# The prologue of a DiT block: modulation by channel pairs, with four projections beside it

## The chip, the core and the metric

The kernel runs on one core of one Trainium2 chip. The metric is the device time of one execution in microseconds; the median of three runs of the kernel before is 1344.03 us (1343.78 to 1344.9). Its engines: PE (TensorE, matmuls into the accumulators in PSUM), ACT (ScalarE), DVE (VectorE), POOL (GpSimd) and SP (SyncE, which here only issues transfers). Each engine works through its own queue in order.

## The reference, cut to what matters

One layer over 1024 latent tokens and 256 context tokens, width 1024, all in float32:

```
m = silu(c) @ w_mod + b_mod          # six vectors of 1024 for the latents; the same with c_ctx for the context
h = rms_norm(x) * g0 * (1 + m[1]) + m[0]
p = h @ w_in                          # 3584 columns: q, two gates, v, g (512 each), and 2 x 512 for the recurrent group
# four HGRN2 heads of 128 columns, eight RG-LRU blocks, output projection, residual, SwiGLU, residual
```

Only m[0] (shift) and m[1] (scale) are needed before the first projection; they come from the first 2048 columns of w_mod. The other four vectors come later.

## The kernel before

Tokens are cut into three blocks: block 0 and 1 of 512 latent tokens, block 2 of the 256 context tokens. Channels are cut into eight k-tiles of 128. A float32 product at fp32r speed is done as three matmuls (`mm3`): both operands are split into a high and a low part (`split`: a cast on ACT, a subtraction on DVE), and hi x hi, hi x lo and lo x hi are added in PSUM. PSUM has eight accumulators: four of tag mm (`ps_mm`) and four of tag px (`ps_x`).

The prologue has these steps, with their lines:

- `load_wm` (L188 to L191) loads k-tile k of the 2048 columns of w_mod as two transfers of 512 KB, three tiles deep. The order on SP is written out by hand (L193 to L207): two k-tiles, block 0 of x, the other k-tiles with the nine small parameter vectors between them, then a tile of w_in, x of block 1, a second w_in tile, the context, the masks.
- L208 to L217: for each k-tile and each quarter of 512 columns, wm is split (L123, L124) and multiplied by `c4`, whose four columns are the high and low parts of the two silu'd vectors; four accumulators `pm` stay open over all k-tiles. The last k-tile is done by plain fp32 matmuls with `c2` (L211).
- `norm_x(b)` (L170 to L176): per 128 tokens a Square with sum on ACT, mean and root (DVE, POOL), a scaling on DVE. `turn(b, k)` (L178 to L183) transposes a k-tile of a block on PE, four transposes for a block of 512. Block 0 is evacuated into `xa` by ACT (L221).
- L225 to L259: the parameters of the recurrent group and of the gates (a chain of small operations on DVE, with three activations on ACT, called the lambda chain below).
- L261 to L275: `pm` is copied to `mrow`, 16 small transposes (L269) bring it into columns, and bias and gain are added: `mcol`.
- L276 to L287: for each block and k-tile, high part `hh` (ACT, L285), full value `hf` (DVE, L286), low part `hl` (DVE, L287).

`inproj(c0, blocks, evac)` (L151 to L160) then does 128 columns of w_in for some blocks: `prep_w` loads and splits the weights (`raw`, `whi`, `wlo`), 24 matmuls a block go into one accumulator, and `evac` takes it out. Head 0 asks for q (blocks 0 and 1), two gates and v (blocks 0, 1, 2). From there on the modulation rows of the later stages (`mod_rows`) are done in small steps on DVE with a sum over partitions by a matmul with ones (L304).

Apart from the order on SP, and one on DVE at the very end, the order on each engine comes from the planner of the tile framework: it takes instructions by program order as priority, places a later one earlier when by its own costs the earlier would have to wait, and puts tiles into free buffers of their tag. `manual_schedule(engines=...)` keeps the instructions traced inside it in the written order on the named engines.

Of the kernel before, what the change touches and what calls it, by code (L numbers as in the profile page):

```python
# [48 lines left out]
def block_kernel(ctx: ExitStack, tc: tile.TileContext, x, c, cx, c_ctx, w_mod, b_mod, norm_g, w_in, lb_logits, gnorm,  # L49
# [45 lines left out]
    # silu of the two conditioning vectors, as columns (k-tile, vector)  # L95
# [6 lines left out]
    c2 = const.tile([P, KD, 4], F32, name="c2")  # L102
    V.memset(c2[:, :, 2:4], 0.0)
    V.tensor_mul(c2[:, :, 0:2], cs.rearrange("p (v k) -> p k v", v=2), cc.rearrange("p (v k) -> p k v", v=2))
    c4 = const.tile([P, KD, 4], F32R, name="c4")
    S.activation(c4[:, :, 0:2], c2[:, :, 0:2], AF.Copy)
    V.tensor_sub(c4[:, :, 2:4], c2[:, :, 0:2], c4[:, :, 0:2].bitcast(F32))
# [26 lines left out]
    # ------------------------------------------------------------------ modulation, norm, input projection, mixers  # L134
# [7 lines left out]

    def prep_w(c0):
        raw = wpool.tile([P, KD, P], F32, tag="raw", name="raw", bufs=2)
        SP.dma_start(raw, w_in[:, c0:c0 + P].rearrange("(k p) f -> p k f", p=P))
        hi = wpool.tile([P, KD, P], F32R, tag="whi", name="whi", bufs=2)
        lo = wpool.tile([P, KD, P], F32R, tag="wlo", name="wlo", bufs=2)
        split(hi, lo, raw)
        prepped[c0] = hi, lo
# [12 lines left out]
    with pool("st") as st:  # L162
# [22 lines left out]
        pm = [ps_mm() for _ in range(4)]  # L185
        wms = []

        def load_wm(k):  # L188
            wms.append(st.tile([P, 2, D], F32, tag="wm", name="wm", bufs=3))
            for n in range(2):  # L190
                SP.dma_start(wms[k][:, n, :], w_mod[k * P:(k + 1) * P, n * D:(n + 1) * D])  # L191

        with tc.manual_schedule(engines={nc.sync.engine}):  # L193
            load_wm(0)
            load_wm(1)
            load_x(0)
            for k in range(2, KD):
                load_wm(k)
                for dst, src in small[2 * k - 4:2 * k - 2]:
                    SP.dma_start(dst, src)  # L200
            prep_w(0)
            load_x(1)
            prep_w(HW_)
            load_x(2)
            mk = st.tile([P, 7 * P], F32, name="mk")
            SP.dma_start(mk, masks)
        for k in range(KD):  # L207
            for n in range(4):  # L208
                wk = wms[k][:, n // 2, n % 2 * 512:(n % 2 + 1) * 512]
                if k == KD - 1:  # L210
                    PE.matmul(pm[n][:4, :], c2[:, k, :], wk, start=(k == 0), stop=(k == KD - 1))  # L211
                    continue
                wh = st.tile([P, 512], F32R, tag="wmh", name="wmh", bufs=3)
                wl = st.tile([P, 512], F32R, tag="wml", name="wml", bufs=3)
# [3 lines left out]
        norm_x(0)  # L218
        xa = st.tile([P, KD, 512], F32, name="xa")
        for k in range(KD):  # L220
            S.activation(xa[:, k, :], turn(0, k), AF.Copy)  # L221
        pt = ps_x()
        PE.transpose(pt[:, :NR], rows, ident[:NR, :NR])
        V.tensor_copy(cols, pt[:, :NR])

        # 8 * log_sigmoid(lambda)
        la = const.tile([P, 8], F32, name="la")
        lg = const.tile([P, 8], F32, name="lg")
        ls = const.tile([P, 8], F32, name="ls")
        ls2 = const.tile([P, 8], F32, name="ls2")  # L230
        lp = const.tile([P, 8], F32, name="lp")
        S.activation(la, col("lam", 0, 8), AF.Abs)
        S.activation(lg, la, AF.Sigmoid, scale=-1.0)
        V.tensor_scalar(ls, lg, -1.0, 2.0, op0=ALU.mult, op1=ALU.add)
        V.reciprocal(ls, ls)
        V.tensor_mul(ls, ls, lg)
        V.tensor_mul(ls2, ls, ls)
        V.tensor_scalar_mul(lp, ls2, 1.0 / 17.0)
        for n in (15, 13, 11, 9, 7, 5, 3):
            V.scalar_tensor_tensor(lp, lp, 1.0 / n, ls2, op0=ALU.add, op1=ALU.mult)  # L240
        V.scalar_tensor_tensor(lp, lp, 1.0, ls, op0=ALU.add, op1=ALU.mult)
        V.tensor_scalar_min(la, col("lam", 0, 8), 0.0)
        V.scalar_tensor_tensor(la, lp, -2.0, la, op0=ALU.mult, op1=ALU.add)
        loga = const.tile([P, 8], F32, name="loga")
        nloga = const.tile([P, 8], F32, name="nloga")
        V.tensor_scalar_mul(loga, la, 8.0)
        V.tensor_scalar_mul(nloga, la, -8.0)

        # lower bounds: softmax over the depth axis, cumulated, less its first layer
        lbe = const.tile([P, 8], F32, name="lbe")  # L250
        lbr = const.tile([P, 8], F32, name="lbr")
        lb = const.tile([P, 8], F32, name="lb")
        omlb = const.tile([P, 8], F32, name="omlb")
        V.tensor_sub(lbe, col("lb", 0, 8), col("lb", 0, 8))
        S.activation(lbe, lbe, AF.Exp)
        V.reciprocal(lbr, lbe)
        V.tensor_mul(lbe, lbe, lbr)
        V.tensor_sub(lb, lbe, lbe)
        V.tensor_scalar(omlb, lb, -1.0, 1.0, op0=ALU.mult, op1=ALU.add)  # L259

        mrow = st.tile([4, 2 * D], F32, name="mrow")  # L261
        for n in range(4):
            if n % 2:
                V.tensor_copy(mrow[:, n * 512:(n + 1) * 512], pm[n][:4, :])
            else:
                S.activation(mrow[:, n * 512:(n + 1) * 512], pm[n][:4, :], AF.Copy)
        pt = ps_x()
        for j in range(16):
            PE.transpose(pt[:, 4 * j:4 * j + 4], mrow[:, j * P:(j + 1) * P], ident[0:4, 0:4])  # L269
        mcol = st.tile([P, 16, 2], F32, name="mcol")  # L270
        ptv = pt[:, 0:64].rearrange("p (j h v) -> p j h v", h=2, v=2)
        V.tensor_copy(mcol, ptv[:, :, 1, :])
        V.tensor_add(mcol, mcol, ptv[:, :, 0, :])
        V.tensor_add(mcol, mcol, col("bm", 0, 16).unsqueeze(2).to_broadcast([P, 16, 2]))
        V.scalar_tensor_tensor(mcol[:, 8:16, :], mcol[:, 8:16, :], 1.0, col("g0", 0, 8).unsqueeze(2).to_broadcast([P, 8, 2]),  # L275
                               op0=ALU.add, op1=ALU.mult)  # L276
        for b in range(3):
            n = BL[b][1]
            v = b // 2
            if b:  # L280
                norm_x(b)
            for k in range(KD):
                src = turn(b, k) if b else xa[:, k, :]
                hf = st.tile([P, 512], F32, tag="hf", name="hf", bufs=3)
                S.activation(hh[b][:, k, :], src, AF.Identity, bias=mcol[:, k, v:v + 1], scale=mcol[:, 8 + k, v:v + 1])  # L285
                V.tensor_scalar(hf[:, :n], src, mcol[:, 8 + k, v:v + 1], mcol[:, k, v:v + 1], op0=ALU.mult, op1=ALU.add)  # L286
                V.tensor_sub(hl[b][:, k, :], hf[:, :n], hh[b][:, k, :].bitcast(F32))  # L287
# [66 lines left out]
    def rg_gates():  # L354
        # two diagonal blocks to a channel tile
# [94 lines left out]
    # ---------------- HGRN2 heads  # L450
    def hg_unit(h):
# [40 lines left out]
        # context state of both directions  # L492
# [24 lines left out]
        # intra-chunk scores by a binary tree over the chunk  # L517
# [41 lines left out]
        # chunk states  # L559
# [67 lines left out]
    with pool("rgp", "right") as cur[0]:  # L627
# [3 lines left out]
        for t in range(4):  # L631
            # gate; then the next tile's convolution goes before this one's scans
# [18 lines left out]
    for k in range(KD):  # L651
        # the mixers' rows, RG-LRU first
# [444 lines left out]
```

## Time and profile before

| | |
|---|---|
| median of three runs | 1344.03 us |
| profiled execution, span from first to last instruction | 1342.8 us |
| PE busy / DVE / ACT | 1294.6 / 978.2 / 655.3 us |
| SP's queue moved | 150.63 MB of 153.57 |

The profiled execution's own time is not listed beside its span; against the median there are 1.2 us around the span. PE's busy share is near full in all of the 40 slices but the first two and the last. In the views below, "busy" of a line is the time of its instructions on their engine, and "idle before, releaser" says what ended the engine's waiting. PEclk is the granted clock of TensorE, 1.00 at 2.4 GHz.

### The profile page before, as it was taken

The page shows a single profiled execution, that of the slowest core. Times are in us where ns is not written, and L with a number is a line of the kernel's source. Part 1 is how long each engine was busy: PE and PEld are TensorE (multiplying, and loading weights), DVE is VectorE, ACT ScalarE, POOL GpSimd, SP SyncE. Part 2 cuts the span into 40 slices and gives each one's busy share as a digit, 9 for nine tenths or more (in the row PEclk, how much of TensorE's full clock was granted, in tenths as well). Part 3 has the DMA queues.
Part 4 walks back from the last instruction along what each step waited for, and adds up shares of the span by engine and source line. Part 5 has one row for each costly group of instructions (what it writes and reads, how often), then busy time and mean ns, then how long its engine had stood idle before and what let it go on. Part 6 is the DMA issues. An engine that isn't in the chain of part 4 may idle for free.

```text
span 1342.8 us, 17344 instructions
## 1 busy us (share of the span) xinstructions
PE 1294.6 (96%) x6271; PEld 1050.8 (78%) x6271; DVE 978.2 (73%) x1609; ACT 655.3 (49%) x1168; POOL 37.7 (3%) x69
## 2 busy tenths in 40 slices
PE   6899999999999999999999999999999999999997
PEld 2587877888888877777887788888888888888886
DVE  5888769738467789874569867777666677896695
ACT  7762443534525777845767333333323334454552
POOL 0100000000000000000010000000000000000000
PEclk8899999999999999999999999999999999999999
DMA  8644042210101011166450532333233215953363
GB/s 301 217 155 160 26 149 64 80 33 17 32 17 32 17 48 47 55 209 206 132 166 25 172 96 88 100 118 110 86 112 104 91 71 188 384 158 95 101 212 102
DMA packets 112896, 153.57 MB, mean 114 GB/s; under 512 B 9469, under 2 KB 69218, under 8 KB 112810
## 3 DMA queue, kind: packets, MB, share of 16 engines
q1 hardware_dynamic: 112250, 150.63, 34.4%
q0 software_dynamic: 560, 1.84, 0.4%
q8 instruction: 49, 0.80, 0.3%
q14 instruction: 37, 0.30, 0.1%
HBM read 119.64 MB, written 32.80 MB: 114 GB/s over the span
## 4 chain that ended last, share of the span: by engine, by line
PE 77%; DVE 12%; ACT 6%; issue 2%; DMA 2%; POOL 1%; SPq 0%; POOLq 0%; DVEq 0%; ACTq 0%
PE mm L129 15%; PE mm L127 15%; PE mm L128 15%; PE px L127 7%; PE px L129 7%; PE px L128 7%; PE px L542 3%; DVE ii L443 1%; DMA raw<-in_w_out 1%; PE px L581 1%; DVE ii L435 1%; DVE a L430 1%; PE mm L217 1%; DVE th L431 1%; PE px L566 1%
## 5 line engine op out<-in xcount | busy, mean ns | idle before, releaser
L123 ACT ACTIVATE wh<-r 128x512 fp32r<-128x512 f32 x160 | 100.9, 633 | 250.8 <-PE mm L128 130.6
L127 PE MATMUL mm<-hh,whi 128*128 128x512 f32 (+1 forms) x576 | 216.1, 376 | 2.8 <-ACT hh L285 2.8
L128 PE MATMUL mm<-hl,whi 128*128 128x512 f32 (+1 forms) x576 | 214.8, 373 | 0.4 <-DVE hl L287 0.4
L129 PE MATMUL mm<-hh,wlo 128*128 128x512 f32 (+1 forms) x576 | 213.9, 374 | 1.0 <-DVE wlo L124 1.0
L127 PEld LDWEIGHTS mm<-hh,whi 128*128 128x128 f32 x576 | 109.2, 190 | 24.2 <-issue 4.3
L129 PEld LDWEIGHTS mm<-hh,wlo 128*128 128x128 f32 x576 | 109.2, 190 | 18.9 <-issue 1.7
L128 PEld LDWEIGHTS mm<-hl,whi 128*128 128x128 f32 x576 | 109.3, 190 | 17.3 <-DVE hl L287 1.4
L124 DVE TENSOR_TENSOR wl<-r,wh 128x512 fp32r<-128x512 f32 x160 | 108.9, 684 | 2.2 <-ACT wh L123 2.0
L123 ACT ACTIVATE gh<-gr 128x512 fp32r<-128x512 f32 x74 | 46.4, 630 | 78.7 <-PE px L128 33.1
L124 DVE TENSOR_TENSOR gl<-gr,gh 128x512 fp32r<-128x512 f32 x74 | 50.6, 687 | 34.8 <-ACT gh L123 34.7
L542 PEld LDWEIGHTS px<-ww,kl 128*128 128x128 f32 x448 | 55.9, 188 | 16.4 <-ACT kl L539 14.7
L542 PE MATMUL px<-ww,kl 128*128 128x128 f32 x448 | 62.0, 281 | 5.2 <-ACT kl L539 5.0
L539 ACT ACTIVATE kl<-ww 128x512 f32<-128x512 f32 x56 | 37.4, 668 | 59.8 <-DVE ww L554 52.2
L128 PE MATMUL px<-wl,gh 128*128 128x512 f32 x164 | 63.9, 390 | 0.0
L127 PE MATMUL px<-wh,gh 128*128 128x512 f32 x164 | 63.8, 389 | 0.0
L129 PE MATMUL px<-wh,gl 128*128 128x512 f32 x164 | 63.8, 389 | 0.0
L118 POOL TENSOR_TENSOR rs<-ms,neg_half 128x1 f32<-128x1 f32 (+1 forms) x42 | 32.3, 780 | 802.2 <-DVE ms L116 648.9
L128 PE MATMUL mm<-wol,omh 128*128 128x512 f32 x128 | 50.6, 396 | 1.7 <-DVE wol L124 1.7
L124 DVE TENSOR_TENSOR wl<-wd,wh 128x512 fp32r<-128x512 f32 x74 | 50.2, 685 | 2.8 <-ACT wh L123 2.4
L123 ACT ACTIVATE wh<-wd 128x512 fp32r<-128x512 f32 x74 | 45.4, 620 | 13.6 <-DVE wd L965 10.0
L127 PE MATMUL mm<-woh,omh 128*128 128x512 f32 x128 | 51.1, 399 | 0.9 <-ACT woh L123 0.9
L127 PE MATMUL mm<-wh,gh 128*128 128x512 f32 x132 | 51.3, 389 | 0.0
(345 smaller groups left out, 3157.2 us busy)
## 6 DMA issues: line engine op xcount, KB each, us to landing
gr<-g_d SPq DMA_DIRECT2D x74, 256.0 KB
og<-in_w_mod SPq DMA_DIRECT2D x64, 256.0 KB
raw<-in_w_in SPq DMA_DIRECT2D x28, 512.0 KB
r<-in_w_ffn_gate SPq DMA_DIRECT2D x22, 512.0 KB
r<-in_w_ffn_up SPq DMA_DIRECT2D x22, 512.0 KB
g_d<-q SPq DMA_DIRECT2D x40, 256.0 KB
wm<-in_w_mod SPq DMA_DIRECT2D x16, 512.0 KB
g_d<-g SPq DMA_DIRECT2D x29, 256.0 KB
```

The costliest lines, as they stand in the source:

```text
L118: G.tensor_tensor(rs[:, :width], ms[:, :width], neg_half[:, :width], op=ALU.pow)
L123: S.activation(hi, src, AF.Copy)
L124: V.tensor_sub(lo, src, hi.bitcast(F32))
L127: PE.matmul(ps, lh, rh, start=first, stop=False)
L128: PE.matmul(ps, lh, rl, start=False, stop=False)
L129: PE.matmul(ps, ll, rh, start=False, stop=last)
L217: PE.matmul(pm[n][:4, :], c4[:, k, :], w, start=(k == 0 and i == 0), stop=(k == KD - 1 and i == 1))
L430: V.tensor_mul(a2, rr[d][:, h], rr[d][:, h])
L431: V.scalar_tensor_tensor(tt[d][:, h], a2, 1.0, tt[d][:, h], op0=ALU.add, op1=ALU.mult)
L435: V.tensor_mul(xx[d], xx[d], tt[d])
L539: S.activation(kl.rearrange("p (j h r) -> p j h r", h=2, r=m), view(w, 1024, [(4 * m, nb), (2 * m + 1, 2), (2, m)]), AF.Copy)
L542: PE.matmul(pl[:, i * P:(i + 1) * P], kl[:, i * P:(i + 1) * P], view(w, i * 256, [(4 * m, 64 // m), (2 * m + 1, 2), (2, m)]), start=True, ...
```

## The change

The w_mod part is cut by output channels instead of k-tiles: chunk c holds 256 channels of shift and the same 256 of scale, all eight k-tiles of them (2 MB, two tiles deep). A chunk needs eight fp32 matmuls, `mods(c)`: k-tile k uses 32 stationary columns (`c32`: the two vectors and 30 zeros) and writes PSUM partitions 32 (k mod 4) to 32 (k mod 4) + 31. ACT copies the accumulator out; four matmuls with `sel`, a matrix that adds the four groups, bring it into columns (`mod_cols`). So two k-tiles of shift and scale are complete after each chunk.

While chunks come in, block 0 of four projections (q, both gates, v of head 0: `FIRST`) is accumulated k-tile by k-tile in the four mm accumulators (`part`), held, and handed to `inproj` when it is called (`held`). The weights of the third and fourth projection lie in the staging pool and are not kept: they are loaded and split again for the other blocks. Order on SP: x of block 0, chunk 0, four w_in tiles, chunk 1, context, chunks 2 and 3, x of block 1, masks. PE, ACT and DVE are put in program order up to the normalisation of block 1. The nine small loads go to ACT's queue. Half of the xa copies go to DVE. The third and fourth w_in tile, as loaded, and the masks use buffers of the x tiles; the squares of norm_x are written into `hh`. The lambda chain is unchanged, and stands between the loop and norm_x(1).

```diff
+        if c0 in held:
+            evac(0, held.pop(c0))
+            blocks = blocks[1:]
         if c0 not in prepped:
             prep_w(c0)
...
-                jk = st.tile([P, D], F32, tag="jk", name="jk")
+                jk = hh[b].rearrange("p k n -> p (k n)")[:, 0:D]
...
-        def load_wm(k):
-            wms.append(st.tile([P, 2, D], F32, tag="wm", name="wm", bufs=3))
-            for n in range(2):
-                SP.dma_start(wms[k][:, n, :], w_mod[k * P:(k + 1) * P, n * D:(n + 1) * D])
+        def load_wm(c):
+            wms.append(st.tile([P, KD, 2, 2 * P], F32, tag="wm", name="wm", bufs=2))
+            for s in range(2):
+                SP.dma_start(wms[c][:, :, s, :], w_mod[:, s * D + 2 * c * P:s * D + 2 * (c + 1) * P].rearrange("(k p) f -> p k f", p=P))
+        FIRST = (0, HW_, 2 * HW_, 3 * HW_)
+        for dst, src in small:
+            S.dma_start(dst, src)
         with tc.manual_schedule(engines={nc.sync.engine}):
+            load_x(0)
             load_wm(0)
+            raws = [load_w(c0, st if n > 1 else wpool) for n, c0 in enumerate(FIRST)]
             load_wm(1)
+            load_x(2)
+            load_wm(2)
+            load_wm(3)
             load_x(1)
+            mk = st.tile([P, D], F32, tag="xt", name="xt", bufs=6)[:, 0:7 * P]
             SP.dma_start(mk, masks)
-        for k in range(KD):
-            for n in range(4):
...
-                split(wh, wl, wk)
-                for i, w in enumerate((wh, wl)):
-                    PE.matmul(pm[n][:4, :], c4[:, k, :], w, start=(k == 0 and i == 0), stop=(k == KD - 1 and i == 1))
...
+        def mods(c):
+            pm = ps_x()
+            for k in range(KD):
+                g = k % 4 * 32
+                PE.matmul(pm[g:g + 32, :], c32[:, k, :], wms[c][:, k, :, :].rearrange("p s n -> p (s n)"), start=(k < 4), stop=(k >= 4))
+            mrow = st.tile([P, 512], F32, tag="hf", name="hf", bufs=3)
+            S.activation(mrow, pm, AF.Copy)
+            return mrow
+        def mod_cols(c, mrow):
+            pt = ps_x()
+            for g in range(4):
+                PE.matmul(pt[:, 2 * g:2 * g + 2], mrow[:, g * P:(g + 1) * P], sel, start=True, stop=True)
+            V.tensor_add(mc[:, :, 2 * c:2 * c + 2, :], pt[:, 0:8].rearrange("p (s k v) -> p s k v", s=2, k=2), bm(c))
...
+        def part(k, cols_):
+            for c0 in cols_:
+                hi, lo = (early if c0 in early else prepped)[c0]
+                mm3(held[c0], hi[:, k, :], lo[:, k, :], hh[0][:, k, :], hl[0][:, k, :], k == 0, k == KD - 1)
+        with tc.manual_schedule(engines={nc.tensor.engine, nc.scalar.engine, nc.vector.engine}):
+            norm_x(0)
...
+            mod_cols(0, mods(0))
+            for c0 in FIRST:
+                held[c0] = ps_mm()
+            for n, c0 in enumerate(FIRST):
+                split_w(c0, raws[n], *((st, early) if n > 1 else (wpool, prepped)))
+                if n == 0:
+                    normed(0, 0, xa[:, 0, :])
+                    normed(0, 1, xa[:, 1, :])
+            for c in range(4):
+                part(2 * c, FIRST)
+                if c < 3:
+                    mrow = mods(c + 1)
+                part(2 * c + 1, FIRST[:2])
+                if c < 3:
+                    mod_cols(c + 1, mrow)
+                    for k in (2 * c + 2, 2 * c + 3):
+                        normed(0, k, xa[:, k, :])
+                part(2 * c + 1, FIRST[2:])
+                if c == 0:
+                    norm_x(2)
...
+            norm_x(1)
+            for k in range(KD):
+                normed(1, k, turn(1, k))
+        for k in range(KD):
+            normed(2, k, turn(2, k))
```

## Rows read from the trace of the kernel before

**Rows 1.** The page, part 1: busy us, share of the span, instructions.
```profile
PE 1294.6 (96%) x6271; PEld 1050.8 (78%) x6271; DVE 978.2 (73%) x1609; ACT 655.3 (49%) x1168; POOL 37.7 (3%) x69
```

**Rows 2.** Stretches: width, each engine's busy time, granted clock, DMA share, GB/s.
```profile
0.00:60.00 60.00, 42.63 (x161) 20.98 (x161) 42.95 (x105) 47.16 (x80) 7.24 (x14) 0.89 0.80 290
60.00:114.00 54.00, 54.00 (x284) 43.84 (x283) 46.86 (x86) 29.38 (x51) 0.00 (x0) 1.00 0.49 156
```

**Rows 3.** Groups of PE up to 60 us: busy, mean ns; idle before, releaser.
```profile
L217 PE MATMUL mm<-wml,c 128*4 128x512 f32 x28 | 12.4, 470 | 0.7 <-DVE wml L124 0.2
...
L269 PE MATMUL px<-ident,mrow 4*128 4x4 f32 x16 | 1.1, 199 | 0.9 <-ACT mrow L266 0.9
```

**Rows 4.** Timeline: start us, us, instruction; the fp32 matmuls of the modulation.
```profile
35.62 3.60 PE L211 MATMUL mm<-wm,c 128*4 128x512 f32 x8
```

**Rows 5.** Timeline of PE over the later matmuls of head 0's projections.
```profile
81.73 0.40 PE L127 MATMUL mm<-hh,whi 128*128 128x512 f32 x1
81.96 0.40 PE L128 MATMUL mm<-hl,whi 128*128 128x512 f32 x1
...
109.50 1.02 PE L304 MATMUL px<-acc,ones 128*1 128x512 f32 x2
...
112.59 0.28 PE L129 MATMUL mm<-hh,wlo 128*128 128x256 f32 x1
```

**Rows 6.** Timeline at the start: first large transfers and their first use.
```profile
1.93 1.77 SPq L191 DMA_DIRECT2D wm<-in_w_mod  x4
...
5.94 0.63 ACT L123 ACTIVATE wmh<-wm 128x512 fp32r<-128x512 f32 x1 [1.98 <-DMA wm<-in_w_mod]
```

**Rows 7.** Stretches of 2 us with full DMA, for transfers of different row lengths.
```profile
8.00:10.00 2.00, 2.00 (x7) 0.54 (x5) 1.70 (x3) 1.49 (x3) 0.00 (x0) 1.00 1.03 418
...
700.50:702.50 2.00, 2.00 (x11) 1.65 (x10) 1.65 (x4) 1.99 (x3) 0.00 (x0) 1.00 1.03 322
...
550.00:552.00 2.00, 2.00 (x13) 1.73 (x13) 1.66 (x2) 1.81 (x4) 0.00 (x0) 1.00 0.98 291
```

**Rows 8.** Timeline of norm_x(0): a Square, means and a scaling.
```profile
13.17 0.15 DVE L116 TENSOR_SCALAR ms<-ss 128x1 f32<-128x1 f32 x1
13.17 1.06 ACT L174 ACTIVATE jk<-xt 128x1024 f32<-128x1024 f32 x1
...
14.00 0.75 DVE L176 TENSOR_SCALAR xt<-xt,rs 128x1024 f32<-128x1024 f32 x1 [0.67 <-POOL rs L118]
...
14.67 0.15 DVE L116 TENSOR_SCALAR ms<-ss 128x1 f32<-128x1 f32 x1
```

**Rows 9.** Stretches of 2 us: the granted clock (third from the end).
```profile
46.00:48.00 2.00, 2.00 (x6) 1.58 (x5) 2.00 (x8) 2.00 (x4) 0.00 (x0) 0.50 1.04 348
...
50.00:52.00 2.00, 2.00 (x9) 1.33 (x7) 2.00 (x4) 1.94 (x5) 0.00 (x0) 0.80 0.32 84
```

**Rows 10.** The chain of waits: start us, us, what; four transposes at either clock.
```profile
22.50 0.85 PE px L182 x4
...
60.92 0.48 PE px L182 x4
```

**Rows 11.** Groups of ACT and DVE up to 66 us: busy, mean ns.
```profile
L221 ACT ACTIVATE xa<-px 128x512 f32<-128x512 f32 x8 | 4.5, 592 | 2.1 <-PE px L182 2.0
...
L287 DVE TENSOR_TENSOR hl<-hf,hh 128x512 fp32r<-128x512 f32 x13 | 8.6, 684 | 0.0
...
L286 DVE TENSOR_SCALAR hf<-px,mcol 128x512 f32<-128x512 f32 x6 | 4.6, 802 | 0.0
L286 DVE TENSOR_SCALAR hf<-xa,mcol 128x512 f32<-128x512 f32 x8 | 4.1, 542 | 0.0
...
L124 DVE TENSOR_TENSOR wlo<-raw,whi 128x1024 fp32r<-128x1024 f32 x2 | 2.4, 1212 | 0.0
```

**Rows 12.** Timeline of DVE: two dependent operations on 8 columns.
```profile
38.33 0.17 DVE L258 TENSOR_TENSOR lb<-lbe 128x8 f32<-128x8 f32 x1
...
38.53 0.17 DVE L259 TENSOR_SCALAR omlb<-lb 128x8 f32<-128x8 f32 x1
```

More of the change, by code (lines that the diff above doesn't have):

```diff
@@ L101, in block_kernel @@
     S.activation(cs, pt[:, :16], AF.Sigmoid)
[L102 to L107, printed above, removed]
+    c2 = const.tile([P, KD, 2], F32, name="c2")
+    V.tensor_mul(c2, cs.rearrange("p (v k) -> p k v", v=2), cc.rearrange("p (v k) -> p k v", v=2))
     cols = const.tile([P, NR], F32, name="cols")
@@ L141, in block_kernel, with load_w, split_w @@
     prepped = {}
-    def prep_w(c0):
[L144 to L149, printed above, removed]
+    held = {}
+    def load_w(c0, where):
+        if where is wpool:
+            raw = wpool.tile([P, KD, P], F32, tag="raw", name="raw", bufs=2)
+        else:
+            raw = where.tile([P, D], F32, tag="xt", name="xt", bufs=6).rearrange("p (k f) -> p k f", k=KD)
+        SP.dma_start(raw, w_in[:, c0:c0 + P].rearrange("(k p) f -> p k f", p=P))
+        return raw
+    def split_w(c0, raw, where, into):
+        hi = where.tile([P, KD, P], F32R, tag="whi", name="whi", bufs=2)
+        lo = where.tile([P, KD, P], F32R, tag="wlo", name="wlo", bufs=2)
+        split(hi, lo, raw)
+        into[c0] = hi, lo
+    def prep_w(c0):
+        split_w(c0, load_w(c0, wpool), wpool, prepped)
     def inproj(c0, blocks, evac):
+        if c0 in held:
+            evac(0, held.pop(c0))
+            blocks = blocks[1:]
         if c0 not in prepped:
@@ L193, in block_kernel @@
+        early = {}
+        FIRST = (0, HW_, 2 * HW_, 3 * HW_)
+        for dst, src in small:
+            S.dma_start(dst, src)
         with tc.manual_schedule(engines={nc.sync.engine}):
+            load_x(0)
             load_wm(0)
+            raws = [load_w(c0, st if n > 1 else wpool) for n, c0 in enumerate(FIRST)]
             load_wm(1)
[L196 to L200, printed above, removed]
@@ L218, in block_kernel @@
-        norm_x(0)
-        xa = st.tile([P, KD, 512], F32, name="xa")
[L220 to L276, printed above, removed]
@@ L277, in block_kernel @@
-        for b in range(3):
+        sel = st.tile([P, 2], F32, name="sel")
+        V.tensor_add(sel, ident[:, 0:2], ident[:, 32:34])
+        V.tensor_add(sel, sel, ident[:, 64:66])
+        V.tensor_add(sel, sel, ident[:, 96:98])
+        c32 = st.tile([P, KD, 32], F32, name="c32")
+        V.memset(c32, 0.0)
+        V.tensor_copy(c32[:, :, 0:2], c2)
+        mcol = st.tile([P, 16, 2], F32, name="mcol")
+        mc = mcol.rearrange("p (s k) v -> p s k v", s=2)
+        xa = st.tile([P, KD, 512], F32, name="xa")
@@ new lines, in bm @@
+        def bm(c):
+            return col("bm", 0, 16).rearrange("p (s k) -> p s k", s=2)[:, :, 2 * c:2 * c + 2].unsqueeze(3).to_broadcast([P, 2, 2, 2])
+        def mods(c):
[6 more added lines that the diff above has]
+            return mrow
@@ L278, in block_kernel, with normed @@
+        def normed(b, k, src):
             n = BL[b][1]
             v = b // 2
-            if b:
-                norm_x(b)
-            for k in range(KD):
[L283 to L287, printed above, removed]
+            hf = st.tile([P, 512], F32, tag="hf", name="hf", bufs=3)
+            S.activation(hh[b][:, k, :], src, AF.Identity, bias=mcol[:, k, v:v + 1], scale=mcol[:, 8 + k, v:v + 1])
+            V.tensor_scalar(hf[:, :n], src, mcol[:, 8 + k, v:v + 1], mcol[:, k, v:v + 1], op0=ALU.mult, op1=ALU.add)
+            V.tensor_sub(hl[b][:, k, :], hf[:, :n], hh[b][:, k, :].bitcast(F32))
```

52 lines of the change are left out of this document (41 added, 11 removed).

## The prediction

> **What bounds the kernel now.** I read the busy times first [rows 1], then two stretches [rows 2], then which groups filled the first of them. TensorE (PE) is busy 96% of the span. From 60 to 114 us it has no gap (54.00 of 54.00 us); in the first 60 us it is busy for 42.63 us, and most of that went to the modulation: twice 28 matmuls, 12.4 us for each set [rows 3], and 3.6 us of fp32 ones [rows 4]. So the change is worth what it makes of this prologue, and I measure it by one milestone: the end of the last matmul of head 0's four projections (q, two gates, v; all three token blocks). Before, that is 112.8 us [rows 5]. PE did two totals of later modulation rows on the way (two instructions each, about 0.95 us a pair), which come later in the new order, so the like figure is 112.8 - 1.9 = 110.9 us. Behind the milestone PE stays dense and the instructions are the same, so I pass its shift on one for one. The span is 1342.8 us and the median 1344.03 us, 1.2 us around it; I add the shift to 1344.0.
>
> **What goes.** 28 casts on ScalarE (ACT) and 28 subtractions on VectorE (DVE), 56 fp32r and 4 fp32 matmuls [rows 3, 4], 16 small transposes [rows 3]. None counts again below; I rebuild the prologue in the new order.
>
> **Loading.** The first 512 KB transfer is issued at 1.93 and used at 5.94 us [rows 6]; block 0's x takes its place. At 418 GB/s [rows 7] each further 0.52 MB needs 1.25 us: x is there at 9.7 us. A chunk of w_mod (2.1 MB) now comes in rows of 256 columns, 1 KB. A stretch in which only FFN weights, also in 1 KB rows, arrived had 322 GB/s, one with w_in in 512 B rows 291 [rows 7]. So a chunk takes 6.5 us and a w_in tile 1.8: chunk 0 at 16.2, four w_in tiles at 23.4, chunk 1 at 29.9, context at 32.4, chunks 2 and 3 at 38.9 and 45.4, block 1 at 50.4 us. At the 4 KB rate all would be earlier, but PE comes to each chunk later than it lands (below), so this costs nothing; if loads were 20% slower still, chunk 2 would land at 47, PE's own time.
>
> **Start to the first projections.** In the fixed order DVE does mean and scaling tile by tile, one per 1.48 us, because each waits for GpSimd (13.17 to 14.67) [rows 8]. Square takes 1.06, with hand-overs some 1.3 [rows 8]; first mean at 7.2, fourth at 11.6, its scaling ends 1.58 later: 13.2. PE has stood still for ten microseconds. A granted clock of 0.50, the lower level of 1.2 GHz, stood from 46 to 48 us with PE busy throughout, and a mean of 0.80 from 50 to 52 [rows 9]; I take the lower level here too, so a transpose takes 0.21 instead of 0.12 us [rows 10]. 32 x 0.21 = 6.7, plus one for the small rows, 0.24: 20.2 us.
>
> **mods(c), the new modulation.** Eight fp32 matmuls of 512 columns. The trace has four such, as eight instructions 0.43 us apart (3.60 us) [rows 4], on four columns of the array; nothing in it shows two matmuls at once. Serial, a chunk costs 16 x 0.43 = 6.9 us. If the four column groups ran fully side by side, 1.7 us. Each fp32 matmul there is two instructions, one behind the other [rows 4]; both halves want the same columns, and the next group's first half stands behind the second. If PE starts matmuls in program order, only neighbours can overlap: 9 x 0.43 = 3.9 us. I take m = 3.9, and keep both ends.
> The Trainium skill, TensorEngine Tiling (Array Packing), Key Properties, says that tiles of the array work independently and can execute matmuls in parallel, and that changing the tiling mode drains the engine; no row here shows either. By its first half a chunk would be the 1.7 us of the rival below.
>
> mods(0) ends at 24.1. Up to the end of part(0), the first of eight k-tiles for four projections, DVE sets the pace: mrow 0.59, four fp32 matmuls with sel (eight instructions, 0.07 each as 16 take 1.1 in [rows 3], 0.6), two small DVE operations 0.36, four splits x 1.21, two normalised k-tiles x (0.54 + 0.68) [rows 11], three matmuls at 0.23 [rows 5], 0.7, hand-overs 0.4: 10.0, so 34.1 us. PE idles for most of it, so I take most of mods(1) at the lower level: seven instructions at 0.86 and two at 0.43, 6.9 us, to 41.0.
>
> **The loop.** Between two mods stand 24 projection matmuls (5.5), sel (0.6) and the wait for the next k-tile's low part (0.8): 6.9. mods(2) begins at 47.9 and ends at 51.8, mods(3) from 58.7 to 62.6. Then 36 matmuls, sel and wait, 9.7: block 0 is through for all four projections at 72.3 us.
>
> **Block 1.** It now follows in program order on ACT and DVE. After mods(3) 5.4 us to the last k-tile of block 0 (68.0), then the lambda chain: 18 dependent operations at 0.20 [rows 12] and three short ones of ACT, 4.0 together (72.0), then norm_x(1): 1.24 + 4 x 1.48 + 0.1 = 7.3, so the first transpose of block 1 is at 79.3. DVE sets the pace from there: 8 x (0.80 + 0.68) [rows 11] + 0.5 = 12.3, to 91.6 us. PE still owes 96 x 0.23 + 72 x 0.12 (256 columns, half of the 0.23) + 58 transposes x 0.12 = 37.7 us; without idling it would end at 110.0. From 72.3 to 79.3 only block 2 can fill (16 transposes and one gate's 24 short matmuls, 4.8 of 7.0); from 79.3 to 91.6, 32 transposes and q's 24 matmuls, 9.3 of 12.3. Idle 2.2 + 3.0 = 5.2: 115.2 us. Shift 115.2 - 110.9 = +4.3: **1348.3 us**.
>
> **Edits that I cost at nothing.** Nine small loads move from SyncE to ACT: at 0.44 us of issue (1.77 for four) [rows 6] 4.0 us, while ACT waits until 5.9 for x anyway; up to 4.0 if that cover went. Every second xa copy moves to DVE (4 x 0.8), under PE's slow transposes. Two w_in tiles are loaded and split a second time (1.21 on DVE each): due near 95 us, but DVE was busy 46.86 of 54 us there [rows 2]; at worst +2.4. The masks wait for an x slot, with those second loads queued behind on SyncE until a transposed block frees it; the weights are due later than that: 0, at worst 2.3 for one late split.
>
> **Rivals.**
> *All four groups at once* (the other side: faster). Place: mods, price 1.7 us instead of 3.9. For it: the four groups write different partitions, so nothing in the data orders them. Against: the paired instructions [rows 4]. mods(0) ends 21.9, part(0) 31.9, mods(1) 35.3 (all at the lower level), mods(2) 43.9, mods(3) 52.5, all behind their chunks. That is 10.1 us earlier than 62.6, and the rest follows: 105.1, shift -5.8, **1338.2**. It decides from m = 3.0 down: m enters four times, once at nearly double cost, 4.6 us per us, and 4.3 / 4.6 = 0.9 below 3.9 is no change. The parallel tiles of the page named above are this case.
> *No overlap.* m = 6.9: mods(0) ends 27.1, part(0) 37.1, mods(1), seven of 16 at the lower level, 7 x 0.86 + 9 x 0.43 = 9.9 later, 47.0, then 13.8 per chunk: mods(3) ends 74.6, 12.0 later than 62.6. Shift +16.3, **1360.3**. For it: every pair of matmuls in this trace starts one after the other.
> *A closed section.* If nothing from outside the fixed order is put between its instructions on ACT, the four finished sums stay in PSUM until block 1 is normalised and PE can only transpose. Then 91.6 + 22.1 + 8.6 + 16 x 0.12 + 1.2 = 125.4, shift +14.5, **1358.5**. For it: the section covers three engines; against: order within it does not forbid others between.
>
> **How the numbers follow.** Overlap by neighbours 0.40, all four 0.33, none 0.17, closed section 0.10. The likeliest gives 1348.3, by itself 1343 to 1353 (idle of 0 to 5 us more or less, the worst cases of the free edits). Within 0.2%, 2.7 us, is what a measurement of this kernel cannot tell from no change. All four: 0.25 faster, 0.05 same, 0.03 slower; neighbours: 0.08, 0.10, 0.22; the other two slower. Faster 0.33, same 0.15, slower 0.52. The range reaches from below the fast rival to above the slow one: 1335 to 1362.
>
> **What would show it.** The matmuls from wm in four bursts: starts 0.43 apart with a burst of 6.9 us means none, 3.9 neighbours, 1.7 all. Part(0) ending near 34 us with DVE full before it; mods(3) ending near 62.6; an idle PE from about 72 to 79 us and half-used until 92; block 1's Squares only after the lambda chain. The prediction is wrong if PE is dense from 60 us on, or if q's block 1 starts before 75 us.

## The result and the profile after

The changed kernel takes 1355.63 us (median of 4 runs, 1354.86 to 1357.65). The kernel before, run beside it, took 1344.47 us. The ratio is 1.0072, 95% interval 1.0052 to 1.0092: slower, 11.2 us by the medians. The span grew from 1342.8 to 1353.8 us. The prediction said 1348.3, slower at 0.52, range 1335 to 1362: the direction and the range held, and the step of +4.3 us was too small by 7.

The page, part 1, of the changed kernel (answers to [rows 1]): PE has nearly the same work in a longer span.

```profile
PE 1294.1 (96%) x6287; PEld 1055.0 (78%) x6287; DVE 968.5 (72%) x1592; ACT 641.4 (47%) x1139; POOL 36.2 (3%) x69
```

The two stretches of [rows 2], of the changed kernel; columns as there (width, busy times, granted clock, DMA share, GB/s):

```profile
0.00:60.00 60.00, 44.58 (x220) 29.63 (x221) 26.99 (x70) 24.50 (x37) 3.52 (x10) 0.94 0.88 282
60.00:114.00 54.00, 38.96 (x175) 29.47 (x174) 44.60 (x85) 31.57 (x52) 2.21 (x4) 0.78 0.44 138
```

and two stretches of 4 us in it:

```profile
84.00:88.00 4.00, 0.69 (x2) 0.29 (x2) 3.83 (x10) 2.89 (x6) 0.00 (x0) 0.50 0.00 0
88.00:92.00 4.00, 3.18 (x8) 2.51 (x9) 3.85 (x6) 4.00 (x9) 0.00 (x0) 0.50 0.40 120
```

The first 60 us hold a little more PE work than before, and DVE is relieved there (26.99 instead of 42.95 us). The loss is in the second stretch: PE stands still for 15 of 54 us in which it had no gap before, and for part of the rest its granted clock is at the lower level (0.50, 1.2 GHz, in both stretches of 4 us; PE had been idle for much of the time before).

The new modulation, as PE ran it; the timeline (start, length, instruction):

```profile
13.05 5.96 PE L192 MATMUL px<-ident,xt 128*128 128x128 f32 x29 [1.00 <-DVE xt L186]
...
19.00 1.92 PE L238 MATMUL px<-wm,c 128*32 128x512 f32 x16
...
31.22 2.29 PE L238 MATMUL px<-wm,c 128*32 128x512 f32 x16
...
40.67 1.92 PE L238 MATMUL px<-wm,c 128*32 128x512 f32 x16
...
49.77 1.92 PE L238 MATMUL px<-wm,c 128*32 128x512 f32 x16
...
61.31 0.39 PE L125 MATMUL mm<-hh,wlo 128*128 128x512 f32 x1
```

A chunk takes 1.92 us, not 3.9: all four column groups ran at once. mods(3) ends at 51.7 us, and PE is through block 0 of all four projections at 61.7 (the last line), about the times of the fast rival (52.5 and 62.2). Up to here the change does what it is for.

What follows, from ACT's and DVE's timelines (each line with what ended the engine's idle time):

```profile
60.49 0.21 ACT L324 ACTIVATE lbe<-lbe 128x8 f32<-128x8 f32 x1 [2.83 <-DVE lbe L323]
60.60 1.04 ACT L184 ACTIVATE hh<-xt 128x1024 fp32r<-128x1024 f32 x1
...
67.29 0.75 DVE L186 TENSOR_SCALAR xt<-xt,rs 128x1024 f32<-128x1024 f32 x1 [0.73 <-POOL rs L114]
...
79.44 0.69 DVE L258 TENSOR_TENSOR hl<-hf,hh 128x512 fp32r<-128x512 f32 x1
...
86.87 0.54 DVE L257 TENSOR_SCALAR hf<-px,mcol 128x256 f32<-128x256 f32 x1
...
87.44 0.60 ACT L505 ACTIVATE tmp<-mm 128x512 f32<-128x512 f32 x1 [0.54 <-DVE hf L257]
```

and from PE's:

```profile
88.82 0.79 PE L123 MATMUL mm<-hh,whi 128*128 128x512 f32 x1 [3.81 <-DVE q L506]
89.41 0.63 PE L124 MATMUL mm<-hl,whi 128*128 128x512 f32 x1
89.83 0.63 PE L125 MATMUL mm<-hh,wlo 128*128 128x512 f32 x1
...
124.81 0.28 PE L125 MATMUL mm<-hh,wlo 128*128 128x256 f32 x1
```

Read it backwards. PE's first projection matmul of block 1 (88.82) waits for q's evacuation to free an accumulator. The evacuation (L505, 87.44) waits for the last k-tile of block 2 on DVE (86.87); block 1's last was done at 80.1. Block 1's normalisation in turn began only when the last of the lambda chain's activations on ACT was through (60.49, the Square at 60.60). The first matmuls then start some 0.43 us apart, at the lower clock. The milestone, the last matmul of head 0's projections, ends at 125.1 us; the end in [rows 5] is 112.59 + 0.28 = 112.9. It comes 12.2 us later, of which 11.0 are left in the span.

### The profile page after: what moved, and what is told of

Its sections match the earlier page's. It is cut to its first block, busy times and chain, and to the rows that moved or that the text cites. A ratio compares the mean times of both kernels' runs of the same rounds, so it can differ in the third digit from the quotient of the medians.

```text
span 1353.8 us, 17287 instructions
## 1 busy us (share of the span) xinstructions
PE 1294.1 (96%) x6287; PEld 1055.0 (78%) x6287; DVE 968.5 (72%) x1592; ACT 641.4 (47%) x1139; POOL 36.2 (3%) x69
## 4 chain that ended last, share of the span: by engine, by line
PE 77%; DVE 12%; ACT 6%; issue 2%; DMA 2%; POOL 1%; POOLq 0%; SPq 0%; DVEq 0%; ACTq 0%
PE mm L123 15%; PE mm L125 15%; PE mm L124 15%; PE px L123 7%; PE px L125 7%; PE px L124 7%; PE px L588 3%; DVE ii L489 1%; PE px L627 1%; DVE hf L257 1%; DVE hl L258 1%; DVE ii L481 1%; DVE a L476 1%; DMA raw<-in_w_out 1%; DVE th L477 1%
## 5 line engine op out<-in xcount | busy, mean ns | idle before, releaser
L124 PE MATMUL mm<-wl,gh 128*128 128x512 f32 x132 | 51.3, 389 | 0.0
L125 PE MATMUL mm<-wh,gl 128*128 128x512 f32 x132 | 51.3, 389 | 0.0
```

The lines of the kernel that those rows point to most:

```text
L124: PE.matmul(ps, lh, rl, start=False, stop=False)
L125: PE.matmul(ps, ll, rh, start=False, stop=last)
```

## Experiments

Theories: **A**, the fixed order itself, lambda chain and norm_x(1) behind the loop, is what costs. **B**, PE stands still because all four accumulators hold finished sums, whose evacuations stand on ACT and DVE behind the normalisation of blocks 1 and 2. **C**, DVE's pace over those 16 k-tiles bounds, whatever the order. **D** and **E** came up on the way: what is won is lost again further on, to the transfers of the later modulation rows and to DVE (D), or to the second splits of two weight tiles and to a total of these rows in PE's queue (E). The expectations of experiments 2 and 4 were written before these letters had settled: there B stands for memory that the normalisation still uses, and in experiment 2 A for the evacuation held back by the fixed order. Every ratio is to the kernel before, run beside it. Its 95% interval is 0.1 to 0.2% either way, some 2 us; where two of the kernels below differ by less, it is the traces that tell them apart.

**1. The column groups.**

```diff
-                g = k % 4 * 32
-                PE.matmul(pm[g:g + 32, :], c32[:, k, :], ..., start=(k < 4), stop=(k >= 4))
+                PE.matmul(pm[0:32, :], c32[:, k, :], ..., start=(k == 0), stop=(k == KD - 1))
...
-                PE.matmul(pt[:, 2 * g:2 * g + 2], mrow[:, g * P:(g + 1) * P], sel, ...)
+                PE.matmul(pt[:, 2 * g:2 * g + 2], mrow[0:32, g * P:(g + 1) * P], sel[0:32, :], ...)
```

> Change: all eight k-tiles of a chunk go to the same column group (32 columns), one after the other, and the gather uses those 32 rows alone. If the short burst of 1.92 us is the four groups side by side: each burst takes 16 x 0.43 = 6.9 us, four bursts some 20 us more, of which what lies under loading and under DVE's pace (mods(0), mods(1)) hides up to 5; time 1367 to 1376. If a matmul with 32 columns were short by itself, whatever the groups: bursts stay near 1.9 us and the time within 2 us of 1355.6.

(`sel`, not shown, then only picks the two rows of the one group.) Measured 1377.19 us, ratio 1.0237 (1.0221 to 1.0253), 21.6 us above the changed kernel and 1 above the first reading. PE's timeline, the second burst:

```profile
34.62 7.05 PE L235 MATMUL px<-wm,c 128*32 128x512 f32 x16
```

7.05 instead of 1.92 us: the parallel groups are real, and worth some 5 us a chunk. That all eight k-tiles also go into one place of PSUM here is not what slows them down: the four matmuls of [rows 4] went into four accumulators, in the same columns of the array, and took 3.60 us for eight instructions, 0.45 each.

**2. The fixed order ends after the loop.**

```diff
-            la = const.tile([P, 8], F32, name="la")    # inside manual_schedule
+        la = const.tile([P, 8], F32, name="la")        # outside, to the end of normed(1, k)
```

> Change: the fixed order on PE, ACT and DVE ends after the loop over chunks; the lambda chain, the normalisation of block 1 and its eight k-tiles are left to the planner. Theory A (the fixed order holds the evacuation of q's sum back on ACT and DVE until block 1 is normalised): the evacuation of q moves from 87.4 to about 62-66 us, PE's first projection matmul of block 1 from 88.8 to about 71, last matmul of head 0 some 8 to 10 us earlier, about 1346. Theory B (the evacuation's tiles lie in memory that block 2's normalisation still uses, so the order alone changes nothing): q's evacuation stays after 85 us, time within 2 us of 1355.6. Theory C (DVE's pace over 16 normalised k-tiles alone): also within 2 us, but with the evacuation early.

Measured 1350.02 us, ratio 1.0037 (1.0024 to 1.0050), 5.6 below the changed kernel. From ACT's and PE's timelines, and the stretch (columns as in [rows 2]):

```profile
80.86 0.60 ACT L505 ACTIVATE tmp<-mm 128x512 f32<-128x512 f32 x1 [1.83 <-DVE hf L257]
...
82.68 0.79 PE L123 MATMUL mm<-hh,whi 128*128 128x512 f32 x1 [4.26 <-DVE q L506]
```

```profile
60.00:92.00 32.00, 21.04 (x85) 14.62 (x84) 26.71 (x47) 16.96 (x28) 0.00 (x0) 0.73 0.32 102
```

Neither theory's numbers. The planner put the lambda chain and norm_x(1) into gaps of DVE and ACT, its last scaling ends at 60.7 instead of 68.0 us, so all comes 6 us earlier; but q's evacuation still follows the last k-tile of block 2. So A, as worded above, is about half of the loss; what holds the evacuation is not the fixed order.

**3. Lambda chain behind block 1, fixed order kept.**

```diff
+            norm_x(1)
+            for k in range(KD):
+                normed(1, k, turn(1, k))
             la = const.tile([P, 8], F32, name="la")
...
-            norm_x(1)
-            for k in range(KD):
-                normed(1, k, turn(1, k))
```

> The changed kernel, the lambda chain traced behind block 1's normalisation instead of ahead of it, still in the fixed order. If the chain (57.2 to 60.5 us on DVE) is what holds norm_x(1) back: block 1's Squares begin near 56.5 instead of 60.6 and all behind comes 3 to 4 us earlier, 1351 to 1353. If only the evacuation behind blocks 1 and 2 counts and the lambda chain just moves ahead of it: within 1.5 us of 1355.6.

Measured 1353.41 us, ratio 1.0060 (1.0045 to 1.0075): 2.2 us below the changed kernel, with intervals that overlap, and just above the first reading. From ACT's and PE's timelines:

```profile
83.27 1.28 ACT L505 ACT_TABLE_LOAD   x1
84.56 0.60 ACT L505 ACTIVATE tmp<-mm 128x512 f32<-128x512 f32 x1
...
85.94 0.79 PE L123 MATMUL mm<-hh,whi 128*128 128x512 f32 x1 [6.24 <-DVE q L506]
```

Block 1's last k-tile is done on DVE at 74.4 us instead of 80.1, so the chain did hold norm_x(1) back. But its operations now lie between block 2's k-tiles, which end at 83.4, and ACT loads a function table before the evacuation. Of 5.8 us PE gets 2.9: the chain's cost was in part moved and not taken away, and 2.2 us is not its price.

**4. Two sums held instead of four.**

```diff
-        FIRST = (0, HW_, 2 * HW_, 3 * HW_)
+        FIRST = (0, HW_)
```

> Change: only two projections of block 0 (q and the first gate) lie beside the modulation, so two of four PSUM accumulators stay free. Theory B (all four held sums, freed only when memory of the normalisation is free, keep PE from block 1): PE starts projections of block 0 for the other two, then block 1, without waiting for q's evacuation; PE idles less between 62 and 92 us, last matmul of head 0 4 to 10 us earlier, 1346 to 1352. Theory C (DVE's pace): PE has 48 matmuls (11 us) more left at 61.5 us, and they fill what stands idle; the end is the same or up to 2 us later, 1354 to 1358. Against both: if the two free accumulators are taken by sums that cannot be evacuated either, nothing changes.

Measured 1359.51 us, ratio 1.0108 (1.0093 to 1.0123): above both readings. With two accumulators free PE did start block 1 early (69.4 us), as B says, and was full from 68 to 84 us. Then it stood again, for the same wait and for a total of the later rows; the 48 matmuls taken out from under the loading were not won back:

```profile
84.00:88.00 4.00, 1.61 (x11) 1.12 (x8) 4.00 (x10) 3.65 (x6) 0.00 (x0) 1.00 0.00 0
```

and PE's timeline:

```profile
89.61 0.58 PE L123 MATMUL mm<-hh,whi 128*128 128x256 f32 x1 [4.00 <-DVE q L506]
...
102.79 1.68 PE L350 MATMUL px<-acc,ones 128*1 128x512 f32 x2 [3.20 <-DVE acc L378]
```

**5. What holds the evacuation: memory or place in the queue?** In the program as built (no view shows it), the tile that q's evacuation writes lies over the 128 bytes of the modulation columns, whose last reader is block 2's last k-tile. The wait of experiment 2 fits: the evacuation's releaser is `hf` at L257, which reads them.

```diff
-        mcol = st.tile([P, 16, 2], F32, name="mcol")      # on top of experiment 2
+        mcol = const.tile([P, 16, 2], F32, name="mcol")
```

> As e1, and the small tile with the modulation columns (128 bytes a partition) lies outside the staging memory, so that the first evacuation tile no longer lies over it; its wait is then for the last k-tile of block 0 alone, but on ACT it still stands behind blocks 1 and 2. Theory B1 (the place in ACT's and DVE's queue holds it): q's evacuation still near 81 us, time within 1.5 us of e1's 1350.0. Theory B2 (the wait for the memory holds it, and its place would come earlier once it is gone): evacuation before 70 us, 1340 to 1344.

Measured 1348.71 us, ratio 1.0021 (1.0011 to 1.0030): 1.3 below experiment 2, with intervals that overlap, as B1 says. ACT's timeline:

```profile
80.46 0.59 ACT L505 ACTIVATE tmp<-mm 128x512 f32<-128x512 f32 x1
```

Nothing is waited for any more, and it is no earlier: it stands behind blocks 1 and 2 in ACT's queue. Why the planner puts it there was not tried.

**6. Free two accumulators by a copy.** On top of experiment 2 (free order), and alone on the changed kernel (fixed order). A pool `onp`, opened ahead of the staging pool, holds the two copies and later the head's `on` tiles.

```diff
+            for c0 in FIRST[:2]:
+                t = onp.tile([P, 4, P], F32, tag="on", name="on", bufs=2).rearrange("p c t -> p (c t)")
+                S.activation(t, held[c0], AF.Copy)
+                held[c0] = t
```

> As e1 (fixed order ends after the loop), and two of the four finished sums (q, first gate) are copied by ACT (2 x 0.55 us) into two tiles that lie outside the staging memory and later hold the head's outputs; their evacuation reads the copies. Theory B (PE stands still because all four accumulators are held until the evacuations, which stand on ACT and DVE behind all of blocks 1 and 2): two accumulators are free at about 64 us, PE has 48 projection matmuls (11 us) of block 1 to do between 66 and 83, the clock stays up, last matmul of head 0 about 9 us earlier than in e1, 1340 to 1343, below the kernel before. Theory C (DVE's pace over the 16 k-tiles alone): the same 48 matmuls come out of the time behind 83 us all the same, but PE then waits again; no more than 3 us, 1347 to 1350.

> The changed kernel with its fixed order, and only the two copies of e7a. Theory B: PE works on block 1 from about 70 us on (when its first k-tile is normalised) instead of 88.8, with 11 us of matmuls under the normalisation; 1345 to 1348, 8 to 10 us below the changed kernel. Theory A (the fixed order is what costs): 1353 to 1356.

Free order: 1344.64 us, ratio 0.9994 (0.9985 to 1.0004), 5.4 below experiment 2, between the two readings. Fixed order: 1353.82 us, ratio 1.0062 (1.0047 to 1.0077), 1.8 below the changed kernel, inside A's reading. The free kernel's stretches and PE's two large waits:

```profile
60.00:92.00 32.00, 27.20 (x134) 22.22 (x133) 26.54 (x47) 22.31 (x39) 0.00 (x0) 0.89 0.32 105
92.00:130.00 38.00, 33.64 (x186) 26.64 (x184) 31.67 (x56) 14.57 (x26) 0.00 (x0) 0.96 0.65 208
```

```profile
83.65 0.58 PE L123 MATMUL mm<-hh,whi 128*128 128x256 f32 x1 [4.13 <-DVE q L511]
...
115.58 0.41 PE L558 MATMUL px<-ident,kc 128*128 128x128 f32 x2 [3.48 <-DVE kc L551]
```

B holds: PE is dense from 64 to 79.5 us. But 11 us of matmuls done early bring 5.4, because PE then waits for the next accumulator, and once more at 112 us, where DVE stands at a row still on its way. In the fixed order the time is A's, but the trace is B's:

```profile
73.69 1.14 PE L123 MATMUL mm<-hh,whi 128*128 128x512 f32 x2
...
93.64 0.58 PE L123 MATMUL mm<-hh,whi 128*128 128x256 f32 x1 [4.63 <-DVE q L511]
...
104.92 1.47 PE L355 MATMUL px<-acc,ones 128*1 128x512 f32 x2 [3.04 <-DVE acc L383]
```

PE begins block 1 at 73.7 instead of 88.8 us, and is full until 88. Then it waits for the next accumulator, and later for a total of the later rows, so nearly all is lost again. This run's time does not decide between A and B.

**7. Block 2 earlier.** Alone on the changed kernel; then with experiment 6 in the free order.

```diff
+                for k in ((), (0, 1, 2), (3, 4, 5), (6, 7))[c]:    # at the end of each pass of the loop
+                    normed(2, k, turn(2, k))
...
-        for k in range(KD):
-            normed(2, k, turn(2, k))
```

> The changed kernel with its fixed order; alone the eight k-tiles of block 2 are normalised inside the loop (three in its second pass, three in the third, two in the last), where DVE stood idle for some 10 of 16 us (40 to 56 us), instead of behind block 1. Theory B (q's evacuation, and with it PE's block 1, waits on ACT and DVE for the last normalised k-tile, whichever that is): the evacuation comes right behind block 1's last k-tile, at about 81 instead of 87.4 us, PE's block 1 at 82 instead of 88.8; 1348 to 1350, 6 to 7 us below the changed kernel. Theory C (the 16 k-tiles' DVE time or the work of PE is only moved): within 2 us of 1355.6. Theory A (fixed order as such): within 2 us of 1355.6.

> Free order after the loop, two sums copied out (e7a) and block 2 normalised in the loop (e9). Theory B: the idle 4 us of PE at 80 to 84 us in e7a, and the half clock behind it, go: 4 to 6 us below e7a's 1344.6, 1338.5 to 1341. Theory D (behind 80 us the kernel is now bound by DVE and the later modulation rows, whose loads start at about 69 instead of 50 us): PE is idle further on instead, as in e7a at 112 us; 1342 to 1345.

Alone: 1357.11 us, ratio 1.0087 (1.0071 to 1.0103); no gain, and as a test a miss. DVE's and ACT's timelines show why:

```profile
75.06 0.75 DVE L186 TENSOR_SCALAR xt<-xt,rs 128x1024 f32<-128x1024 f32 x1 [0.73 <-POOL rs L114]
...
87.40 0.81 DVE L257 TENSOR_SCALAR hf<-px,mcol 128x512 f32<-128x512 f32 x1
...
88.24 0.60 ACT L505 ACTIVATE tmp<-mm 128x512 f32<-128x512 f32 x1 [2.88 <-DVE hf L257]
```

In the written order five of the eight k-tiles stood behind mods(3) and ran from 57 to 64.6 us, and the last two of them waited for PE, where their transposes stand behind all of part(7). So they pushed the lambda chain and norm_x(1) back by 7.8 us (the last scaling, 75.06 instead of 67.29), more than the 7.3 that block 2 took behind block 1. The evacuation again follows the last k-tile, whichever it is. Together with the copies: 1345.28 us, ratio 1.0004 (0.9993 to 1.0016), no better than experiment 6, close to the second reading. Where PE stood now:

```profile
87.73 1.86 PE L355 MATMUL px<-acc,ones 128*1 128x512 f32 x2 [5.08 <-DVE acc L383]
```

**8. The rows' loads earlier.** On top of the last: the w_mod tiles lowest in the staging pool, the masks through one of their buffers.

```diff
+        wm0 = wm_tile()                                  # ahead of load_x(0)
...
-            mk = st.tile([P, D], F32, tag="xt", name="xt", bufs=6)[:, 0:7 * P]
+            mk = wm_tile().rearrange("p k s n -> p (k s n)")[:, 0:7 * P]
...
+        V.tensor_copy(mask.rearrange("p a b -> p (a b)"), mk)    # now ahead of norm_x(1)
         norm_x(1)
```

> As e10, and the masks go through a buffer of the w_mod tiles (free from about 43 us on) instead of an x tile, and these tiles lie lowest in the staging memory, so that the memory of the later modulation rows is free when the last chunk's loads end. The rows' first loads go out at about 55 us instead of 69. Theory D: PE no longer waits near 112 us for VectorE, which waited for a row; 2 to 4 us below e10. If the rows never held PE up: within 1 us of e10.

Measured 1345.09 us, ratio 0.9994 (0.9984 to 1.0003), within 1 us of the one before, though the rows' first load goes out at 59.3 instead of 71.1 us: the rows' loads did not hold PE up. From ACT's and PE's timelines:

```profile
87.40 1.09 ACT L119 ACTIVATE whi<-raw 128x1024 fp32r<-128x1024 f32 x1
...
88.11 1.86 PE L360 MATMUL px<-acc,ones 128*1 128x512 f32 x2 [4.54 <-DVE acc L388]
89.91 0.80 PE L123 MATMUL mm<-hh,whi 128*128 128x512 f32 x1
```

PE's next work, the third projection, needs weights that are split a second time, and on ACT that split stands behind 16 evacuation steps; in front of it in PE's queue is the total of a row that is not yet summed.

**9. Second splits and totals.** On top of experiment 8.

```diff
-                if k == 2 and todo:
+                if k == 6 and todo:
...
         inproj(h * P, (0, 1), ev_q)
+        if h == 0:
+            prep_w(2 * HW_)
...
             inproj((1 + d) * HW_ + h * P, (0, 1, 2), ev_z)
+            if h == 0 and d == 0:
+                prep_w(3 * HW_)
```

> As e11, with the second split of the third and fourth projection's weights traced ahead of the evacuations that it now stands behind (on ACT at 87.4 us in e11, the third projection's first matmul of block 1 right behind it), and the totals of the later modulation rows traced four rows later, so that PE does not stand at one from 83.4 to 88.1 us. Theory E (in e10 and e11 what the early accumulators gave was lost again there: two splits that the prediction counted as free, and a total of the rows in PE's queue): third projection's block 1 begins near 83.5 instead of 89.9 us, no half clock at 88 to 92; 4 to 7 us below e11, 1338 to 1341. Theory D (bound by DVE and by the rows' transfers behind 80 us): PE is idle further on instead; within 2 us of e11.

Measured 1337.97 us, ratio 0.9943 (0.9929 to 0.9956): 7.1 below experiment 8, 8.0 below the kernel before, E's numbers. C falls: PE is all but full from 60 to 92 us although DVE does the same 16 k-tiles, block 2's now inside the loop. The stretches and PE's first matmul of the third projection in block 1:

```profile
60.00:92.00 32.00, 31.41 (x173) 25.98 (x172) 26.59 (x44) 21.60 (x37) 0.66 (x1) 1.00 0.33 108
92.00:130.00 38.00, 33.78 (x193) 27.85 (x193) 33.36 (x60) 13.60 (x26) 0.00 (x0) 0.96 0.49 159
```

```profile
83.45 0.50 PE L123 MATMUL mm<-hh,whi 128*128 128x512 f32 x1
```

This beats both kernels. How much is the splits' and how much the totals' was not tried apart.

**10. The column groups alone.** The kernel before, with its loading and free order; the four quarters of the columns in the four groups.

```diff
-                wh = st.tile([P, 512], F32R, tag="wmh", name="wmh", bufs=3)
-                wl = st.tile([P, 512], F32R, tag="wml", name="wml", bufs=3)
-                split(wh, wl, wk)
-                for i, w in enumerate((wh, wl)):
-                    PE.matmul(pm[n][:4, :], c4[:, k, :], w, ...)
+                PE.matmul(pm[32 * n:32 * n + 32, :], c32[:, k, :], wms[k][:, n // 2, n % 2 * 512:(n % 2 + 1) * 512],
+                          start=(k == 0), stop=(k == KD - 1))
...
-        for j in range(16):
-            PE.transpose(pt[:, 4 * j:4 * j + 4], mrow[:, j * P:(j + 1) * P], ident[0:4, 0:4])
+        for jj in range(4):
+            PE.transpose(pt[:, jj * P:(jj + 1) * P], mrow[:, jj * P:(jj + 1) * P], ident)
```

> Kernel before, with its loading and its free order, and only the modulation changed: no casts and no split, c in 32 columns with 30 zeros, the four quarters of the 2048 modulation columns in the four column groups of one accumulator, all eight k-tiles summed there, one copy, four full transposes. If the column groups run side by side, eight k-tiles x (8 instructions, about 0.9 us) follow the loads, which end near 30 us, and the modulation columns are there near 32 instead of 42 us; milestone and time 5 to 9 us before the kernel before, 1335 to 1339. If DVE's 8 x 1.48 us for the normalised k-tiles and the loading of x bound it instead: 2 us or less earlier, 1342 to 1344.

Measured 1342.59 us, ratio 0.9979 (0.9970 to 0.9989), 2.6 below the kernel before, inside the second reading's times, if a little more than its 2 us. PE's timeline and a stretch:

```profile
32.32 2.65 PE L212 MATMUL mm<-wm,c 128*32 128x512 f32 x8
36.48 0.65 PE L261 MATMUL px<-ident,mrow 128*128 128x128 f32 x4 [1.52 <-ACT mrow L258]
```

```profile
32.00:36.00 4.00, 2.96 (x11) 0.55 (x9) 1.14 (x7) 3.25 (x6) 0.00 (x0) 0.69 1.06 381
```

The last k-tile comes at 32.3 us, behind the loads, and PE, idle between loads, is partly at the lower clock (0.69): the columns are there near 37, five of the expected ten us earlier. DVE comes to block 1's first k-tile at 56.4 instead of 59.2 us, so about half of these five are lost by then. A gain, but a small one.

## Why the prediction was right in direction and short in size

**m failed.** The step "If PE starts matmuls in program order, only neighbours can overlap" gave 3.9 us a chunk; measured 1.92, and 7.05 without groups (experiment 1). The paired instructions of [rows 4], read as evidence against four at once, said nothing of groups that write different partitions. This alone would have made the forecast 10.1 us too late, so that the kernel came out slower has another cause. The direction was luck to that extent: what made 1348.3 a slower time, m = 3.9, did not happen; what did, all four groups at once with the section closed, had no time of its own, and the closed section a chance of 0.10.

**The overlap under block 1's normalisation failed: the closed section was real, and it was not a rival of the others but came on top.** The main sum lets PE do a gate's 24 short matmuls and q's 24 matmuls before the last k-tile of block 1; no accumulator was free, and PE did no projection matmul from 61.7 to 88.8 us. The prediction gave this 0.10 and priced it with m = 3.9 alone. With the fast rival's m of 1.7 and the section closed, its own numbers give a milestone of 105.1 + (125.4 - 115.2) = 115.3 us. Its mechanism was short in two places. It let the evacuation follow block 1's last k-tile; it followed block 2's, 80.1 to 87.4 us: 7.3. And PE began block 1 at the lower clock: eleven matmuls from 88.82 to 93.58 at 0.43 instead of 0.23, 2.2. The sum, 124.8, stands against 123.2 measured on the prediction's scale (125.1 less 1.9 for two totals); nearly all of the rest is that block 1 was through at 80.1 us, 1.4 before the 81.5 that these numbers imply.

**Its reason was half wrong.** "The section covers three engines" is not what holds the evacuations: with the section ended after the loop they still came last (experiment 2), and with the wait for memory gone as well (experiment 5). They stand behind blocks 1 and 2 in ACT's and DVE's queues. What the section does cost is the 6 us by which x(1), on the chip since 52 us, was normalised later than a free order does it (experiments 2 and 3).

**The steps in between** held: norm done 13.0 (13.2), transposes and rows 19.0 (20.2), block 1's chain from the lambda operations on 57.2 to 68.0 (the prediction's 4.0 and 7.3 us: 11.3; measured 10.8), its k-tiles at 1.45 us (1.48).

**Totals.** That they "come later in the new order" was wrong: two still ran before the milestone, at 105.0 and 121.7 us.

**Free edits.** The masks and the SP queue behind them: the rows' first load went out at 75.5 us, 25 later than before. From 88.8 to the milestone PE waits for nothing in the changed kernel, neither for a row nor for a split, so 0 was right for both there, since PE was late anyway; bringing the loads forward changed nothing in another kernel either (experiment 8). Once PE was not late, the second splits and the totals cost 7.1 us (experiment 9).

**One for one** behind the milestone: 12.2 us there, 11.0 in the span.

Where the expected gain went, in order: 5.6 us to the fixed tail, 5.4 to four held accumulators, 7.1 to second splits and totals that stand in the queues where PE was not expected so early. Each was measured on top of the one before, and in another order the shares differ: in the fixed order the copies gave 1.8. With all three gone the time is 1338.0, the fast rival's 1338.2, so its gain was there to be had; that the two agree so closely is in part chance. What stays open: the 3.2 us for which PE waits until 106.7 us in the kernel of experiment 9 for a weight's low part on DVE, and how much of experiment 9 is the totals'.

## What to carry to other kernels

Work brought forward into held accumulators pays only when each sum's evacuation can also run early: look up where the evacuation stands in ACT's and DVE's queues, and copy a sum out to memory that is free if it stands behind other work. Rivals that can happen together are to be priced together, not given separate chances. When an engine is brought forward, go through its queue for each instruction that others were only just in time for; there the gain is lost first.

## What the runs showed of the hardware

- Four fp32 matmuls into four groups of 32 columns ran side by side, second halves and all: 16 instructions in 1.92 us against 7.05 in one group, a factor of 3.7. The Trainium skill, TensorEngine Tiling (Array Packing), Key Properties, says that different tiles can execute matmuls in parallel, and the trace agrees. It also says that changing the tiling mode drains the engine. No cost above some 0.1 us shows: the next projection matmul starts 1.85 us after the first instruction of the burst at 49.77 us, and the one after it 0.33 us later instead of 0.23, as it also does behind the gather matmuls, which use all columns.
- The four gather matmuls (128 x 2) take 0.95 us as eight instructions, 0.12 each, not 0.07.
- From 12 to 20 us the granted clock of the changed kernel reads 1.00, yet 29 transposes took 5.96 us, 0.205 each, about the length of the slower four in [rows 10], near which the clock read 0.50 to 0.62. From 14 to 18 us PE and its weight loads are both busy throughout, so no wait explains it. The burst right behind took 1.92 us, as at 1.00 later. The cause stays open.
